# A hybrid attention block on one core: first token tile loaded first, products on a tile of zeros ahead of the first real ones, and an order planned anew

## The chip, the cores and the metric

One core of a Trainium2 chip runs the whole layer in one launch. The metric is device time in microseconds (us), the median of three runs. PE is TensorE, ACT ScalarE, DVE VectorE, POOL GpSimd, and SP the SyncE queue, from which all DMAs of this kernel are issued.

## The reference, cut to what matters

The input x has 1024 tokens of width 1024, in float32.

```python
h = rms_norm(x, norm_pre_g)
proj = h @ w_in            # sb_q, sb_k, sb_v, sb_gate, c_q, c_kv, k_rope, mla_gate
sb_o  = stick_breaking_attention(sb_q, sb_k, sb_v)        # 8 heads of 64, strictly causal
sb_y  = head_rms_norm(sb_o) * silu(sb_gate)
mla_o = latent_attention(...)                             # 8 heads, low rank q and kv, rotary part
mla_y = head_rms_norm(mla_o) * silu(mla_gate)
y = concat(sb_y, mla_y) @ w_out
x = x + rms_norm(y, norm_post_g)
x = x + rms_norm(p @ w_ple) * sigmoid(x @ w_ple_gate + b_ple_gate)
```

## The kernel before, in words

**Arithmetic.** Each float32 operand of a large product is split into a rounded high part and the rest, and a product is three PE passes: high by high, high by low, low by high. The products are mostly 128x512. The 1024 tokens are eight tiles of 128.

**The head.** `HEAD` (line 67) lists the first loads: `v0` to `v3` are four slabs of 512 KB of the value columns of `w_in` (`first`, line 936, then `load_split`, line 838, which also splits them), `x0` to `x2` are token tiles of 512 KB, and `g0` is the gain row `norm_pre_g` (4 KB). Lines 984 to 990 spread the gain row over 128 partitions by products with a tile of ones (`PE` into `ps_t`, `ACT.copy` into `gb["pre"]`) and do `x_norm(0)` and `x_tr(0)`. `x_norm` (line 859) is a square with a sum on ACT, a scale on DVE, a power on POOL, then the multiplication by the inverse root and the gain: on DVE alone for tiles below `EARLY` (line 866), on DVE and POOL from there on. `x_tr` (line 873) is eight PE transposes and the split of the result into `hh` and `hl`. `xv_gen` (line 947) then multiplies a token tile by the four slabs: 24 products into one PSUM bank of the three under the tag "a". The products for the queries and keys of the first head pair (`qk0_gen`, line 1027) follow.

**The middle.** `SEQ` (line 60) is the order in which head pairs are worked, `FILL0` (line 61) that of the projections woven between them, `RATES` (line 56) how many of those are spent for each stretch of attention. In `sb_rows` (line 1263) one row tile of the stick-breaking attention takes a product of every second element on POOL if its number `qi` is in `PAIRS` (lines 63 and 1283), otherwise on DVE.

**The tail.** `TAIL` (line 55) is the order of the last stage: `o` is an output projection with its norm, `w` loads and combines the gate weights, `x` and `a` load and transpose the new residual, `e` is the gated step for two token tiles, with seven products of half-size matrices in place of eight.

**How the order is made.** Nothing is issued when it is written down. The `Recorder` (line 333) notes every operation with the tiles that it reads and writes, a priority and a duration by formula (`cost`, line 461). The priority is the place in the recording, plus `SHIFT` of the piece that the operation belongs to (line 387; a piece begins at each `R.piece`), plus `LOW` (line 53) for background work, plus `R.bias` (`-URGENT` in the head, `-AHEAD` for attention scores). `schedule` (line 517) is a list planner: at each step it takes for an engine the ready operation of lowest priority, with `LAT` (line 510) added between a producer and a reader on another engine. It also holds durations doubled for PE until a stretch before was busy enough (lines 660 to 665). `FLIP` (line 224) names operations that are moved to another engine, and `SPLITS` (line 66, read by `choice`) says for groups of operations whether DVE or POOL does them. `issue` (line 698) then emits all operations in the planned order, and each engine works through its own list in that order, whatever the chip does.

The line of nearly all instructions in the profile is L730, in `issue`, so that rows are told apart by their tiles: `t` and `a` are PSUM banks, `u`, `f` and `h` SBUF tiles.

```python
prio=self.turn() + (LOW if self.low else 0) + self.bias
```

Of the kernel before, what the change touches and what calls it, by code (L numbers as in the profile page):

```python
# [15 lines left out]
BF16 = mybir.dt.bfloat16  # L16
# [31 lines left out]
def f(ap):  # L48
# [4 lines left out]
LOW = 336  # L53
TICK = 10240.0 / 3.0
TAIL = ("o4", "w1", "w2", "o5", "a4", "o6", "w3", "x1", "x0", "x2", "e4", "a0", "e0", "a6", "x3", "e6", "a2", "e2")
RATES = (4.934, 9.256, 4.735, 4.518, 3.1, 1.436, 0.789, 0.703, 2.078, 0.654, 0.413, 0.788, 0.259, 0.582, 0.786, 1.784)
URGENT = 56
EARLY = 4
LATER = 5
SEQ = ((0, 0), (1, 0), (6, 0), (4, 0), (7, 0), (2, 0), (0, 1), (3, 0), (3, 1), (2, 1), (5, 0), (7, 1), (5, 1), (4, 1), (1, 1), (6, 1))  # L60
FILL0 = ("x4", "x5", "l0", "x6", "x7", "q1", "c0", "b1", "r3", "t0", "lrv0", "g3", "rope0", "r0", "r1", "g4", "q2", "r2", "q3", "g6", "g0", "g1", "g2", "g7", "ple0", "g5")
N1 = 3
PAIRS = (0, 1, 2, 3)
ON_POOL = (0, 1, 2, 3)
LOWS = ("g", "q", "ple", "x", "b", "c", "t", "l")
SPLITS = (1, 0, 0, 1, 0, 1, 1, 1, 0, 1, 1, 1, 1, 1, 0, 1, 1, 0, 1, 0, 1, 1, 1, 0, 0, 1, 1, 1, 0, 0, 0, 1, 0, 0, 0, 1, 0, 0, 1, 0, 0, 1, 1)
HEAD = ("v0", "x1", "x0", "g0", "v3", "v1", "v2", "x2")
AHEAD = 52

SHIFT = {  # L70
# [662 lines left out]
def block_kernel(ctx, tc, x, p, positions, norm_pre_g, w_in, q_norm_g, w_uq, kv_norm_g, w_ukv,  # L733
# [3 lines left out]
    R = Recorder(nc)  # L737
# [52 lines left out]
    ones = const([1, 128], "ones")  # L790
    POOL.memset(ones, 1.0)
    nhalf = const([128, 8], "nhalf")
    POOL.memset(nhalf, -0.5)
    hpi = const([128, 1], "hpi")
    POOL.memset(hpi, HALF_PI)
    g_sb, g_mla = const([128, 4], "g_sb"), const([128, 4], "g_mla")
# [991 lines left out]
```

## Time and profile before

| what | value |
|---|---|
| median of 3 runs | 774.36 us (774.33 to 775.73) |
| the profiled execution | 774.4 us |
| its span, first to last instruction | 772.6 us |
| PE busy | 754.5 us, 98% of the span |
| DVE / ACT / POOL busy | 81% / 50% / 45% |

The profile is of one execution. Its busy times are unions of the instructions' spans, and matmul ends are modelled, so that a busy PE is not yet a PE at its full rate: the count of instructions in a stretch, or the time of a known number of them, tells the rate. The idle time of an engine is given with what ended it. The profiled execution differs from the median by 0.04 us, and 1.8 us of it lie outside the span.

### The profile page before, as it was taken

Reading aid. Unit: us, or ns where it says so; the run is one execution under the profiler, and the core shown is the slowest. Engines: PE = TensorE matmul, PEld = TensorE weight load, DVE = VectorE, ACT = ScalarE, POOL = GpSimd, SP = SyncE. Lnnn points to the kernel's source line nnn. Section 1 sums busy time; section 2 is a strip of 40 time slices with the busy share of each in tenths; the row PEclk is TensorE's granted clock in tenths of the full one; section 3 lists DMA queues with packets and bytes.
Section 4 is the critical chain, followed back from the end, with each engine's and each line's share of the span. In section 5 each row is a group of like instructions: output and inputs, shape, how many; then the busy total and the mean of one; then the engine's idle time right before and its main releaser. Section 6 shows DMA issues by size and latency. Waiting matters only on the chain.

```text
span 772.6 us, 11778 instructions
## 1 busy us (share of the span) xinstructions
PE 754.5 (98%) x3912; PEld 621.5 (80%) x3912; DVE 624.1 (81%) x1184; ACT 384.9 (50%) x898; POOL 346.6 (45%) x315
## 2 busy tenths in 40 slices
PE   6999999999999999999999899999999999999997
PEld 4887889878788878888788788888888888778886
DVE  5876334499867877788888899999899998888996
ACT  6315123333443586565646768776776642433211
POOL 4445111102312258878884712342275114468664
PEclk9999999999999999999999999999999999999999
DMA  9644460269995844566356588686734475172242
GB/s 329 201 171 139 145 213 5 77 218 354 330 341 190 275 155 143 167 206 189 110 184 225 187 290 260 216 302 223 240 116 154 166 254 178 60 268 87 94 150 82
DMA packets 101966, 148.69 MB, mean 192 GB/s; under 512 B 7441, under 2 KB 55057, under 8 KB 101906
## 3 DMA queue, kind: packets, MB, share of 16 engines
q1 hardware_dynamic: 101906, 147.95, 57.4%
q8 instruction: 31, 0.51, 0.3%
q14 instruction: 29, 0.24, 0.1%
HBM read 101.26 MB, written 46.66 MB: 191 GB/s over the span
## 4 chain that ended last, share of the span: by engine, by line
PE 84%; DVE 7%; DMA 4%; ACT 2%; issue 1%; POOL 1%; SPq 1%; POOLq 0%; ACTq 0%; DVEq 0%
PE a L730 58%; PE t L730 26%; DVE u L730 4%; DVE f L730 2%; ACT u L730 1%; DMA u<-k_d 1%; DMA u<-in_w_ple_gate_dram 1%; DMA u<-q_d 1%; DMA u<-in_x_dram 1%; DMA f<-in_positions_dram 1%; DMA q_d<-f 1%; SPq L730 1%; DVE nm L730 1%; ACT f L730 0%; POOL u L730 0%
## 5 line engine op out<-in xcount | busy, mean ns | idle before, releaser
L730 POOL TENSOR_TENSOR u<-u,u 128x512 f32<-128x512 f32 (+16 forms) x134 | 200.5, 1512 | 153.3 <-DVE u L730 64.0
L730 PE MATMUL a<-h,f 128*128 128x512 f32 x864 | 242.1, 405 | 0.0
L730 PEld LDWEIGHTS a<-h,f 128*128 128x128 f32 x864 | 155.2, 189 | 26.8 <-DVE f L730 0.6
L730 DVE TENSOR_TENSOR u<-t,u 128x512 fp32r<-128x512 f32 (+4 forms) x284 | 150.6, 556 | 13.7 <-ACT u L730 10.0
L730 PE MATMUL t<-u,u 128*128 128x512 f32 (+4 forms) x580 | 154.4, 370 | 1.9 <-DMA u<-q_d 0.5
L730 PE MATMUL a<-u,u 128*128 128x512 f32 (+2 forms) x524 | 136.7, 371 | 0.5 <-DVE u L730 0.5
L730 PE MATMUL t<-ident,u 128*128 128x128 f32 x792 | 125.8, 276 | 2.4 <-DVE u L730 2.4
L730 ACT ACTIVATE u<-t 128x512 f32<-128x512 f32 (+5 forms) x208 | 91.0, 509 | 67.7 <-PE t L730 57.8
L730 PEld LDWEIGHTS t<-u,u 128*128 128x128 f32 x580 | 103.4, 189 | 23.2 <-DVE u L730 4.3
L730 ACT CAST u<-t 128x512 fp32r<-128x512 f32 (+3 forms) x187 | 85.6, 495 | 71.0 <-PE t L730 35.3
L730 PE MATMUL a<-h,u 128*128 128x512 f32 (+1 forms) x492 | 118.3, 390 | 0.4 <-DVE u L730 0.4
L730 PEld LDWEIGHTS t<-ident,u 128*128 128x128 f32 x792 | 97.8, 142 | 24.9 <-DVE u L730 7.0
L730 PEld LDWEIGHTS a<-h,u 128*128 128x128 f32 x492 | 90.0, 188 | 21.3 <-issue 1.0
L730 PEld LDWEIGHTS a<-u,u 128*128 128x128 f32 x524 | 93.1, 188 | 17.2 <-DVE u L730 2.2
L730 ACT ACTIVATE u<-t,nms 128x384 f32<-128x384 f32 (+4 forms) x96 | 55.3, 581 | 42.3 <-DVE nms L730 35.3
L730 DVE TENSOR_TENSOR_SCAN u<-u 128x64 f32<-128x64 f32 (+6 forms) x64 | 59.1, 934 | 20.6 <-ACT u L730 20.4
L730 DVE TENSOR_TENSOR u<-u,u 128x512 f32<-128x512 f32 (+13 forms) x91 | 73.2, 820 | 2.0 <-ACT u L730 1.1
L730 DVE TENSOR_TENSOR u<-a,u 64x512 f32<-64x512 f32 (+4 forms) x75 | 47.8, 649 | 15.6 <-ACT u L730 9.7
L730 DVE TENSOR_REDUCE nm<-t 128x1 f32<-128x384 f32 (+4 forms) x96 | 51.6, 545 | 2.1 <-PE t L730 1.3
L730 POOL TENSOR_TENSOR rs<-ms,nhalf 128x8 f32<-128x8 f32 x16 | 27.7, 1731 | 57.0 <-DVE ms L730 37.5
L730 ACT ACTIVATE f<-a 128x512 bf16<-128x512 f32 (+3 forms) x64 | 34.3, 538 | 36.7 <-PE a L730 32.1
L730 PE MATMUL a<-u,h 128*128 128x512 f32 x192 | 49.8, 406 | 0.0
(110 smaller groups left out, 795.5 us busy)
## 6 DMA issues: line engine op xcount, KB each, us to landing
u<-q_d SPq DMA_DIRECT2D x64, 256.0 KB, 4.7
u<-k_d SPq DMA_DIRECT2D x16, 512.0 KB, 5.3
u<-v_d SPq DMA_DIRECT2D x16, 512.0 KB, 4.5
u<-in_w_ple_gate_dram SPq DMA_DIRECT2D x16, 512.0 KB, 5.4
f<-in_w_in_dram SPq DMA_DIRECT2D x14, 512.0 KB, 5.0
v_d<-u SPq DMA_DIRECT2D x12, 512.0 KB, 4.1
f<-in_x_dram SPq DMA_DIRECT2D x9, 512.0 KB, 4.6
k_d<-u SPq DMA_DIRECT2D x9, 512.0 KB, 3.9
```

The costliest lines, as they stand in the source:

```text
L730: x["fn"](*[place(a) for a in x["args"]], **{k: place(a) for k, a in x["kw"].items()})
```

## The change

The head list begins with `x0` and the gain row. A tile of zeros `still` (128x512, bf16) is set by DVE, and ahead of the head 20 products of it go into a PSUM bank that nothing reads; their priority number is raised by 150, so that the planner puts them where PE has nothing else that is ready. In the planner the delay from a landed DMA to its reader goes from 620 to 900 ns (650 to 950 for PE and POOL). With it all of the order's tables are other ones: `SHIFT` throughout, `FLIP` (225 entries before, 250 after), `TAIL`, `SEQ` (one swap), `FILL0`, `RATES`, `LOW`, `URGENT`, `EARLY`, `AHEAD`, `PAIRS` and `SPLITS` (entries 9, 13, 19 and 22; 13 is not read by any line). The arithmetic of the result is the same.

```diff
-LOW = 336
+LOW = 377
-TAIL = ("o4", "w1", "w2", "o5", "a4", "o6", "w3", "x1", "x0", "x2", "e4", "a0", "e0", "a6", "x3", "e6", "a2", "e2")
-RATES = (4.934, 9.256, 4.735, 4.518, 3.1, 1.436, 0.789, 0.703, 2.078, 0.654, 0.413, 0.788, 0.259, 0.582, 0.786, 1.784)
-URGENT = 56
-EARLY = 4
+TAIL = ("w1", "w2", "w3", "o4", "o5", "x0", "x2", "a4", "o6", "e4", "x1", "a0", "e0", "x3", "a6", "e6", "a2", "e2")
+RATES = (4.934, 9.256, 4.735, 4.518, 3.1, 1.642, 0.698, 0.666, 2.078, 0.654, 0.413, 0.788, 0.304, 0.522, 0.229, 3.217)
+URGENT = 83
+EARLY = 3
-SEQ = (... (5, 0), (7, 1), (5, 1), (4, 1), (1, 1), (6, 1))
-FILL0 = ("x4", "x5", "l0", "x6", "x7", "q1", "c0", "b1", "r3", "t0", "lrv0", "g3", "rope0", "r0", "r1", "g4", ...)
+SEQ = (... (5, 0), (5, 1), (7, 1), (4, 1), (1, 1), (6, 1))
+FILL0 = ("l0", "x4", "x5", "x6", "x7", "q1", "c0", "r3", "b1", "t0", "lrv0", "g3", "g4", "r0", "rope0", "r1", ...)
-PAIRS = (0, 1, 2, 3)
+PAIRS = (0, 1, 3)
-HEAD = ("v0", "x1", "x0", "g0", "v3", "v1", "v2", "x2")
-AHEAD = 52
+HEAD = ("x0", "g0", "v0", "x2", "x1", "v1", "v3", "v2")
+WARM = (20, 150)
+AHEAD = -3
...
-           ("POOL", "DVE"): 65.0, ("POOL", "POOL"): 102.0, ("POOL", "SP"): 55.0, ("SP", "PE"): 650.0,
-           ("SP", "ACT"): 620.0, ("SP", "DVE"): 620.0, ("SP", "POOL"): 650.0, ("SP", "SP"): 620.0}
+           ("POOL", "DVE"): 65.0, ("POOL", "POOL"): 102.0, ("POOL", "SP"): 55.0, ("SP", "PE"): 950.0,
+           ("SP", "ACT"): 900.0, ("SP", "DVE"): 900.0, ("SP", "POOL"): 950.0, ("SP", "SP"): 900.0}
...
+    still = const([128, 512], "still", BF16)
+    DVE.memset(still, 0.0)
...
+    R.piece("warm")
+    R.bias = WARM[1]
+    idle = ps_a()
+    for _ in range(WARM[0]):
+        mm(idle, still[:, 0:128], still, start=True, stop=True)
+    R.bias = 0
     for item in HEAD:
         R.piece(item)
         first(item)
```

## Rows read from the trace of the kernel before

**Rows 1.** The page's first part: busy time, share of the span and instructions of each engine.

```profile
span 772.6 us, 11778 instructions
PE 754.5 (98%) x3912; PEld 621.5 (80%) x3912; DVE 624.1 (81%) x1184; ACT 384.9 (50%) x898; POOL 346.6 (45%) x315
```

**Rows 2.** Busy time by stage: stretch in us, its length, then busy us (instructions) of PE, PEld, DVE, ACT and POOL, the granted clock of PE, the DMA engines' share, GB/s.

```profile
0.00:6.00 6.00, 0.01 (x1) 0.04 (x1) 0.43 (x1) 2.11 (x2) 1.36 (x11) 1.00 0.68 217
6.00:10.50 4.50, 3.74 (x4) 1.12 (x4) 1.71 (x5) 3.57 (x7) 3.89 (x3) 1.00 1.04 407
10.50:15.80 5.30, 5.29 (x20) 4.66 (x21) 5.30 (x8) 3.51 (x6) 0.42 (x1) 1.00 1.02 394
15.80:40.00 24.20, 24.20 (x118) 19.93 (x117) 20.86 (x36) 11.03 (x19) 12.04 (x10) 1.00 0.68 212
40.00:280.00 240.00, 237.64 (x1200) 197.34 (x1199) 160.13 (x374) 91.42 (x242) 61.43 (x72) 1.00 0.60 203
280.00:360.00 80.00, 80.00 (x450) 65.50 (x449) 65.17 (x94) 54.42 (x126) 67.43 (x63) 1.00 0.55 169
360.00:400.00 40.00, 39.25 (x209) 31.62 (x208) 32.96 (x45) 20.00 (x42) 33.80 (x20) 1.00 0.51 166
400.00:440.00 40.00, 38.37 (x211) 31.42 (x210) 35.77 (x61) 26.43 (x65) 24.86 (x23) 1.00 0.58 195
764.75:772.60 7.85, 2.69 (x23) 2.49 (x22) 4.61 (x9) 1.36 (x3) 2.13 (x2) 0.84 0.27 100
```

**Rows 3.** What PE waited for in the whole span (waits of over 0.15 us): us in total, times, longest.

```profile
PE t L730 <- DMA u<-in_norm_pre_g_dram: 6.0, 1, 6.0
PE t L730 <- DVE u L730: 2.8, 5, 1.2
PE a L730 <- DVE u L730: 0.9, 2, 0.5
PE a L730 <- DVE f L730: 0.6, 1, 0.6
PE t L730 <- DVE f L730: 0.6, 2, 0.3
PE t L730 <- DMA u<-q_d: 0.5, 1, 0.5
PE t L730 <- ACT u L730: 0.3, 1, 0.3
PE a L730 <- ACT f L730: 0.3, 1, 0.3
PE t L730 <- DMA u<-k_d: 0.3, 1, 0.3
```

**Rows 4.** Instructions in order of time, 0 to 14 us: start, length, engine, operation, tiles, form, count, and the idle time before with what ended it.

```profile
0.73 0.20 POOL masks.py:197 MEMSET ident<- 128x128 f32 x1 [0.29 <-POOLq L1769]
0.74 0.44 SPq L730 DMA_DIRECT2D u<-in_w_in_dram  x1
1.24 0.46 SPq L730 DMA_DIRECT2D u<-in_x_dram  x1
1.45 0.43 DVE L730 CAST eye<-ident 128x128 bf16<-128x128 f32 x1 [1.45 <-POOL ident masks.py:199]
1.74 0.33 SPq L730 DMA_DIRECT2D u<-in_norm_pre_g_dram  x1
2.12 0.35 SPq L730 DMA_DIRECT2D u<-in_x_dram  x1
5.17 1.04 ACT L730 CAST u<-u 128x1024 fp32r<-128x1024 f32 x1 [3.16 <-DMA u<-in_w_in_dram]
6.44 1.06 ACT L730 ACTIVATE u<-u 128x1024 bf16<-128x1024 f32 x1 [0.22 <-DMA u<-in_x_dram]
7.76 1.06 ACT L730 ACTIVATE u<-u 128x1024 bf16<-128x1024 f32 x1 [0.17 <-DMA u<-in_x_dram]
8.81 0.56 ACT L730 COPY u<-t 128x512 f32<-128x512 f32 x1
9.71 2.63 DVE L730 SCALAR_TENSOR_TENSOR u<-u,sr,u 128x512 f32<-128x512 f32 x3
```

**Rows 5.** The same view for PE alone, 0 to 32 us.

```profile
5.99 3.75 PE L730 MATMUL t<-u,ones 1*128 1x512 f32 x4 [5.99 <-DMA u<-in_norm_pre_g_dram]
10.51 1.97 PE L730 MATMUL t<-ident,u 128*128 128x128 f32 x8 [0.77 <-DVE u L730]
24.05 3.04 PE L730 MATMUL a<-u,h 128*128 128x512 f32 x12
```

**Rows 6.** Busy time of the instructions on the tile `ident` alone (the transposes), in four stretches that each hold eight of them; the columns are PE, PEld, DVE, POOL, granted clock, DMA share, GB/s.

```profile
13.31:15.02 1.71, 1.71 (x8) 1.50 (x7) 0.00 (x0) 0.00 (x0) 1.00 1.05 396
23.27:24.05 0.78, 0.78 (x8) 0.78 (x7) 0.00 (x0) 0.00 (x0) 1.00 0.00 0
```

**Rows 7.** Groups of PE instructions by form from 10.5 to 15.5 us: busy us, mean ns, idle before.

```profile
L730 PE MATMUL a<-u,h 128*128 128x512 f32 x4 | 2.3, 686 | 0.0
```

**Rows 8.** Groups by form over the whole span, POOL and DVE: busy us, mean ns of one, idle before and what ended it.

```profile
L730 POOL TENSOR_TENSOR u<-u,u 128x448 f32<-128x448 f32 x7 | 13.3, 1900 | 2.2 <-ACT u L730 2.2
L730 POOL TENSOR_TENSOR u<-u,u 128x192 f32<-128x192 f32 x4 | 3.0, 748 | 3.2 <-ACT u L730 3.2
L730 DVE TENSOR_TENSOR u<-u,u 128x448 f32<-128x448 f32 x1 | 0.6, 600 | 0.0
L730 DVE TENSOR_TENSOR u<-u,u 128x192 f32<-128x192 f32 x1 | 0.4, 359 | 0.4 <-ACT u L730 0.4
L730 POOL TENSOR_TENSOR u<-u,u 128x1024 f32<-128x1024 f32 x2 | 5.3, 2632 | 2.1 <-DVE u L730 2.1
L730 DVE TENSOR_TENSOR u<-u,u 128x512 f32<-128x512 f32 x35 | 28.9, 842 | 0.6 <-ACT u L730 0.3
L730 DVE TENSOR_TENSOR u<-a,u 128x512 f32<-128x512 f32 x31 | 20.7, 684 | 5.5 <-PE a L730 4.0 <-ACT h L730 1.1 <-ACT u L730 0.2
```

More of the change, by code (lines that the diff above doesn't have):

```diff
@@ L52 @@
 NU, NF = 28, 10
-LOW = 336
+LOW = 377
 TICK = 10240.0 / 3.0
-TAIL = ("o4", "w1", "w2", "o5", "a4", "o6", "w3", "x1", "x0", "x2", "e4", "a0", "e0", "a6", "x3", "e6", "a2", "e2")
-RATES = (4.934, 9.256, 4.735, 4.518, 3.1, 1.436, 0.789, 0.703, 2.078, 0.654, 0.413, 0.788, 0.259, 0.582, 0.786, 1.784)
-URGENT = 56
-EARLY = 4
+TAIL = ("w1", "w2", "w3", "o4", "o5", "x0", "x2", "a4", "o6", "e4", "x1", "a0", "e0", "x3", "a6", "e6", "a2", "e2")
+RATES = (4.934, 9.256, 4.735, 4.518, 3.1, 1.642, 0.698, 0.666, 2.078, 0.654, 0.413, 0.788, 0.304, 0.522, 0.229, 3.217)
+URGENT = 83
+EARLY = 3
 LATER = 5
-SEQ = ((0, 0), (1, 0), (6, 0), (4, 0), (7, 0), (2, 0), (0, 1), (3, 0), (3, 1), (2, 1), (5, 0), (7, 1), (5, 1), (4, 1), (1, 1), (6, 1))
-FILL0 = ("x4", "x5", "l0", "x6", "x7", "q1", "c0", "b1", "r3", "t0", "lrv0", "g3", "rope0", "r0", "r1", "g4", "q2", "r2", "q3", "g6", "g0", "g1", "g2", "g7", "ple0", "g5")
+SEQ = ((0, 0), (1, 0), (6, 0), (4, 0), (7, 0), (2, 0), (0, 1), (3, 0), (3, 1), (2, 1), (5, 0), (5, 1), (7, 1), (4, 1), (1, 1), (6, 1))
+FILL0 = ("l0", "x4", "x5", "x6", "x7", "q1", "c0", "r3", "b1", "t0", "lrv0", "g3", "g4", "r0", "rope0", "r1", "q2", "r2", "q3", "g6", "g0", "g1", "g2", "g7", "ple0", "g5")
 N1 = 3
-PAIRS = (0, 1, 2, 3)
+PAIRS = (0, 1, 3)
 ON_POOL = (0, 1, 2, 3)
 LOWS = ("g", "q", "ple", "x", "b", "c", "t", "l")
-SPLITS = (1, 0, 0, 1, 0, 1, 1, 1, 0, 1, 1, 1, 1, 1, 0, 1, 1, 0, 1, 0, 1, 1, 1, 0, 0, 1, 1, 1, 0, 0, 0, 1, 0, 0, 0, 1, 0, 0, 1, 0, 0, 1, 1)
-HEAD = ("v0", "x1", "x0", "g0", "v3", "v1", "v2", "x2")
-AHEAD = 52
+SPLITS = (1, 0, 0, 1, 0, 1, 1, 1, 0, 0, 1, 1, 1, 0, 0, 1, 1, 0, 1, 1, 1, 1, 0, 0, 0, 1, 1, 1, 0, 0, 0, 1, 0, 0, 0, 1, 0, 0, 1, 0, 0, 1, 1)
+HEAD = ("x0", "g0", "v0", "x2", "x1", "v1", "v3", "v2")
+WARM = (20, 150)
+AHEAD = -3
 SHIFT = {
[151 rows of a table removed]
[159 rows of a table added]
 }
 FLIP = (
[12 rows of a table removed]
[13 rows of a table added]
 )
```

335 rows, old and new, of tables (FLIP, SHIFT) are left out of this document.

## The prediction, made before the changed kernel was run

> **What bounds the kernel now.** I read the engines' totals first: PE is busy 754.5 of 772.6 us, and no other engine over 81% [rows 1]. So there are 18 us at most to take out, plus time in which a busy PE runs below its rate. The stages say where they lie [rows 2]: 6.7 us ahead of 10.5 us, 5.2 us after 764.75 (the last sums and stores, which follow PE's last product), and some 6 us in all between; from 15.8 to 40 us and from 280 to 360 us PE is never idle. The list of PE's waits agrees: 6.0 us for the gain row's DMA at the start, then many short ones, most ended by DVE [rows 3].
>
> The head in order of time [rows 4, 5]: SP issues a weight slab at 0.74, `x1` at 1.24, the gain row at 1.74, `x0` at 2.12. The three loads of 512 KB free their first readers on ACT at 5.17, 6.44 and 7.76: one every 1.3 us, while the DMA engines are full [rows 2]. `x0`, which starts the chain (square, scale, power, multiplication, transposes), is the third of them. Its first transpose runs at 10.51, 2.75 us after its square began.
>
> That PE is busy from 10.5 to 15.8 us hides a second loss. The granted-clock column reads 1.00 there, but eight transposes take 1.71 us at 13.31 and 0.78 us at 23.27 [rows 6], and four 128x512 products 2.3 us against 12 in 3.04 us later [rows 5, 7]. I go by the durations: until about 15.8 us PE works at 1.2 GHz, after that at 2.4. Before the rise it had worked without a break since 10.51; the four products of the gain row (5.99 to 9.74) and the gap of 0.77 us behind them had not brought it.
>
> **The change part by part.**
>
> *Half-rate work made full-rate.* 16 transposes take 1.97 + 1.71 us with waits; I count 2 x (1.71 - 0.78) = 1.9 us [rows 6]. The four products: 2.3 - 4 x 0.25 = 1.3 us, of which about 0.5 is the first ones' wait for operands, so 0.8. If PE is at full rate when it reaches them: **-2.7 us** (bounds 0 and -3.2).
>
> *`x0` first.* It would land where the first load did, 5.17 in place of 7.76, and the same 2.75 us of chain would give a first transpose at 7.9. But the multiplication also needs the gain row's products: their row is there by 5.99, the first half takes two products (1.9 us at half rate, 0.95 at full) and an ACT copy of 0.56, then about 0.75 of DVE [rows 4, 5]: 8.3 to 9.2. So by the data, a gain of 1.3 to 2.2 us.
>
> *The 20 products of zeros.* They wait for a memset on DVE, which can run from 0.73, as the other engines do, so I let them start at 1.2. No row has a 128x512 bf16 product. Bounds for one: 0.25 us (float32r, full rate) and 0.94 (the one-row float32 products) [rows 5]; nearest is the first, doubled while at half rate. As before the rise came after 5.3 us of unbroken work, I put it at 6.5: about 11 products at 0.5 by then, 9 at 0.25, then the gain row's four at 0.47: they would end at 10.7. The Trainium skill (TensorE: Matmul & The Clock Gate, Part 1) gives 0.427 and 0.216 us for a product of this size at the two rates; by these figures the end would be 9.9, an estimate, and no row here shows such a product. PE takes its list in order, so whichever zeros stand ahead of the transposes hold them. Between 8.3 (data) and 10.7 (queue) I take 9.7, nearer to the queue, since nothing else is ready for PE by then and the planner will have put nearly all 20 there: **-0.8 us** (bounds -2.2 and +0.3).
>
> *`x1` later.* It goes from the second 512 KB to about the fifth, so to a landing near 10.3 and transposes near 13. Between 9.7 and there PE has 0.8 us of transposes and some 1.5 us of products with the first slab, and those for `x2`, which lands earlier. I charge **+0.3 us** (bounds 0 and 1.3). Later loads stay in the saturated DMA stream and are not late: PE is the last to finish with them up to 40 us [rows 2].
>
> *Longer DMA delay in the planner.* It moves transfers ahead of their use. The waits it aims at are those for `q_d` and `k_d`, 0.8 us [rows 3]: I take **-0.4 us** (bounds -0.8 and, if it spreads uses apart, +1).
>
> *`PAIRS`.* Products with `qi` 2 go from POOL to DVE: 7 x 1.90 + 4 x 0.75 = 16.3 us less on POOL, 7 x 0.60 + 4 x 0.36 = 5.6 us more on DVE [rows 8]. Most lie between 280 and 440 us, where POOL is up to 84% busy and DVE 81 to 89% [rows 2]. I cost them at nothing: DVE has 26 us free there. If that cover goes they cost up to 5.6 us. The Trainium skill (SBUF — State Buffer, Who interferes with whom) says that a DVE operation with two SBUF inputs and a GpSimd one that reads SBUF hold one port in turn; by that 16.3 us of holding go and 5.6 come, and the edit would be a gain, at most the 2.4 us that PE idles there. The trace leans that way: 0.84 us for two SBUF inputs, 0.68 with one in PSUM [rows 8].
>
> *The rest together, nothing.* `EARLY` puts 2.6 us of POOL behind `x3`, needed only by the fourth token tile; four low parts of gate weights go from DVE to POOL; two splits of small weights change engine: PE waits 1.5 us on such tiles in the whole span [rows 3]. The tail's last three steps are the same, so the 7.85 us after 764.75 stay [rows 2]. `SHIFT`, `FLIP`, `SEQ`, `RATES`: PE's work is the same, and nothing in the trace tells which short wait goes or comes; I take 0, with 4 us to either side.
>
> Sum: -2.7 - 0.8 + 0.3 - 0.4 = -3.6 us on the profiled execution's 774.4, whose difference to the median (774.36) is nothing: **770.8 us**.
>
> **The rivals.**
>
> *A, the new order also closes waits in the middle.* PE waits listed behind the head come to 5.5 us (12.3 less 6.0 and 0.77) [rows 3]. Closing 4 of them beyond the above gives 766.8. For: most are single waits for DVE of under 1.2 us, which another order can remove. Against: nothing in the diff names one.
>
> *B, the zeros stand in the way.* If the clock rises only as the last of them ends (1.2 + 20 x 0.5 = 11.2, then 1.9 us for the gain row), the transposes start at 13.1: 2.6 us later, which returns the 2.7 us: 774.3, the same. Zeros that leave the clock as it is come out near this or, with the transposes at half rate too, some 4 us above it. For: PE's list is in order, and before the clock came late. The Trainium skill (TensorE: Matmul & The Clock Gate, Part 2, step 1) says that only weight loads are pulled ahead, matmuls stay in program order; no row of before has ready work behind waiting products, so none tests it.
>
> *C, slower: DVE becomes the bound between 280 and 440 us.* The 5.6 us moved onto it come out ahead of PE there: 770.8 + 5.6 = 776.4. It decides once PE's waits for DVE in this stretch exceed some 6 us; they are about 2.4 us of idle PE now, all after 360 us. For: DVE ends most of PE's waits. Against: 26 us of free DVE time, and POOL's relief.
>
> **How the numbers follow.** Forecast 0.52 (its own range 768.5 to 772.5, from the head's bounds), A 0.18, B 0.15, C 0.13, and 0.02 for a larger gain than A. A measurement of this kernel can tell about 0.2%, 1.5 us, from no change. Faster: the forecast, A and the rest, 0.72; same: B, 0.15; slower: C, 0.13. The range goes from 766.2, just past A, to 775.6, past B; it leaves out C and a larger gain.
>
> **What would show it.** Right: the first loads' reader on ACT is a square, at about 5.2; products of zeros fill PE from about 1.2; transposes start between 8.3 and 10.7 and eight take 0.8 us from the first; PE has no gap over 0.5 us until 40 us; from there the same products run some 3.5 us earlier. The forecast is wrong if the first eight transposes take 1.7 us, or start after 11 (B), if PE's idle time between 280 and 440 us is over 6 us (C), or if the idle time between 40 and 660 us moves by more than 2 us (A, or an order that fits the chip worse).

## The result, and the profile after

The changed kernel takes **777.76 us** (median of 6 runs, 776.45 to 779.32) against 774.56 (6 runs, 774.02 to 775.73) of the kernel before on the same chip: a ratio of 1.0042, 95% interval 1.0027 to 1.0056. That is 3.2 us slower, where 3.6 us faster was forecast, and outside the range. The profiled execution took 777.18 us, 0.6 less than the median, 775.4 of them in the span. One execution of one experiment below (`a_f0`, 1059 us where its others lie between 776.7 and 780.9) was far slower than the rest and is left out of its ratio.

The totals of after, the lines that answer to [rows 1]:

```profile
span 775.4 us, 11804 instructions
PE 760.4 (98%) x3932; PEld 622.3 (80%) x3932; DVE 636.5 (82%) x1206; ACT 388.9 (50%) x898; POOL 315.6 (41%) x297
```

PE is busy 5.9 us longer. The 20 products of zeros take 7.3 us of it, so the real products take 1.4 us less. DVE has 12.4 us more, POOL 31.0 less.

Stages of after, to set beside [rows 2] (columns as there):

```profile
0.00:6.00 6.00, 4.81 (x12) 1.75 (x13) 0.27 (x1) 2.50 (x3) 1.31 (x11) 1.00 0.67 205
6.00:10.50 4.50, 4.41 (x14) 1.45 (x12) 2.31 (x4) 1.92 (x5) 0.97 (x1) 1.00 1.04 416
10.50:15.80 5.30, 4.41 (x19) 3.02 (x20) 4.90 (x8) 5.30 (x10) 1.07 (x2) 1.00 1.07 359
15.80:40.00 24.20, 23.60 (x117) 18.77 (x116) 23.17 (x36) 12.57 (x24) 16.98 (x10) 1.00 0.70 238
280.00:360.00 80.00, 79.66 (x449) 65.11 (x449) 71.27 (x105) 54.59 (x129) 58.95 (x56) 1.00 0.59 185
400.00:440.00 40.00, 38.39 (x205) 30.68 (x204) 36.10 (x59) 23.67 (x55) 22.88 (x20) 1.00 0.62 199
```

The head is filled (4.81 and 4.41 us busy, where [rows 2] has 0.01 and 3.74), but 1.5 us of idle PE have come between 10.5 and 40 us, where before had none; between 280 and 360 us, the place of rival C, 0.34 us of PE is idle with DVE 89% busy. From 400 to 440 us PE is as busy as before (38.39 and 38.37 us), yet has 205 products to show for it where before has 211 (of mixed sizes): busy time alone does not tell its progress.

Chosen lines of the head of after in order of time (start, length, engine, operation, tiles, form, count, idle time before and what ended it), to set beside [rows 4, 5]:

```profile
0.74 0.44 SPq L740 DMA_DIRECT2D u<-in_w_in_dram  x1
1.19 7.31 PE L740 MATMUL a<-still 128*128 128x512 bf16 x20 [1.19 <-DVE still L740]
1.24 0.45 SPq L740 DMA_DIRECT2D u<-in_x_dram  x1
1.74 0.33 SPq L740 DMA_DIRECT2D u<-in_norm_pre_g_dram  x1
5.08 1.04 ACT L740 CAST u<-u 128x1024 fp32r<-128x1024 f32 x1 [2.76 <-DMA u<-in_w_in_dram]
6.35 1.06 ACT L740 ACTIVATE u<-u 128x1024 bf16<-128x1024 f32 x1 [0.22 <-DMA u<-in_x_dram]
8.43 1.98 PE L740 MATMUL t<-u,ones 1*128 1x512 f32 x4
9.59 0.59 ACT L740 COPY u<-t 128x512 f32<-128x512 f32 x1 [2.08 <-PE t L740]
11.07 1.45 PE L740 MATMUL t<-ident,u 128*128 128x128 f32 x8 [0.66 <-DVE u L740]
12.61 3.60 PE L740 MATMUL a<-u,h 128*128 128x512 f32 x12
13.35 0.43 SPq L740 DMA_DIRECT2D u<-in_w_in_dram  x1
16.14 1.09 PE L740 MATMUL t<-ident,u 128*128 128x128 f32 x8
```

A weight slab is still the first transfer and `x0` the second; `x0`'s square starts at 6.35, and before had one at 6.44. The zeros hold the gain row's products until 8.43 (5.99 in [rows 5]); behind them ACT waits 2.08 us for its copy. The first transpose runs at 11.07, later than the 10.51 of before. The clock is up: eight transposes take 1.45 us with a wait inside, then 1.09, where [rows 5, 6] have 1.97 and 1.71.

PE's waits of after, to set beside [rows 3] (us in total, times, longest):

```profile
PE t L740 <- ACT u L740: 2.0, 5, 0.8
PE a L740 <- DVE still L740: 1.2, 1, 1.2
PE a L740 <- ACT f L740: 1.1, 3, 0.7
PE t L740 <- DMA u<-q_d: 1.0, 1, 1.0
PE t L740 <- DVE u L740: 0.8, 2, 0.7
PE t L740 <- DVE f L740: 0.8, 2, 0.4
PE a L740 <- DVE f L740: 0.7, 2, 0.4
PE a L740 <- ACT u L740: 0.5, 2, 0.3
```

The 6.0 us for the gain row and most of the 2.8 us for DVE `u` are gone. Besides the 1.2 us at the start, until the tile of zeros is set, many short waits stand in their place: 3.6 us of the 6.9 shown are ended by ACT, for which PE had waited 0.6 us in all.

Waits alone don't place the loss, so I also count PE's progress: each real product counts with the median step of its form in before, from its start to the next one's (a 128x512 one 0.233 us; zeros count nothing), summed up to a moment. The lead is that sum minus the sum of before at the same moment, in us; the total of both kernels is some 736. A row is good to some 0.3 us, since whole products are counted, and it is from one profiled execution. Some of these are extremes of their kernel: `a_f0` and `a_f12` were profiled 2.8 and 2.6 us above their medians, `a_q`, `b_f20` and `b_x0b` 1.3 to 1.7 below, which shows in the right-hand columns. Names without a meaning yet are those of the experiments below.

```
                               at 40   200   230   380   480   720   760 us
after                           -0.5   1.1   0.4   1.6  -0.6  -3.1  -3.0
order of after,  a_f0            0.2   2.2  -1.1   0.2  -2.8  -6.2  -6.7
                 a_f12           0.6   2.7  -0.7   0.5  -2.4  -4.9  -5.3
                 a_q             0.9   2.1   2.7   3.8   0.5  -1.7  -1.6
                 a_pairs        -0.2   1.1   0.7   1.5  -1.8  -5.3  -5.7
                 a_ple          -0.2   1.7   0.3   1.5  -1.6  -4.4  -4.3
                 a_norm          0.4   2.1   1.6   2.6   2.5  -0.8  -0.7
order of before, b_f20           1.7   2.9   3.1   2.3   3.0   2.3   2.3
                 b_x0b           1.8   2.4   2.9   3.0   3.7   2.8   2.7
                 b_ple           0.9   0.2   0.7   0.4   1.2   0.5   0.5
                 b_norm          0.9   0.7   0.0   0.0   2.0   2.3   2.3
```

After is behind at 40 us, ahead by 1.6 at 380, and loses 2.2 us up to 480 and 2.5 more up to 720. Runs of one kernel scatter by 0.7 to 8 us, so that a difference of rows is trusted here only where all rows of an order show it. From 380 to 720 us the lead falls by 3.4 to 6.8 in all seven rows of after's order. In those of before's order, with the four profiles that are not in the table (`b_f11`, `b_split`, `b_pairs`, `b_x0`), it moves by no more than some 1.2 either way, and by 2.3 upward in `b_norm`, which does less work. At 40 us, on the other hand, a difference under 1 us means little: `b_ple` and `b_norm` have the head of before unchanged and are 0.9 ahead there, with 24 products between 10.5 and 15.8 us where before had 20.

### The profile page after: what moved, and what is told of

Read it like the earlier page. It is cut to its first block, busy times and chain, and to the rows that moved or that the text cites. A ratio compares the mean times of both kernels' runs of the same rounds, so it can differ in the third digit from the quotient of the medians.

```text
span 775.4 us, 11804 instructions
## 1 busy us (share of the span) xinstructions
PE 760.4 (98%) x3932; PEld 622.3 (80%) x3932; DVE 636.5 (82%) x1206; ACT 388.9 (50%) x898; POOL 315.6 (41%) x297
## 4 chain that ended last, share of the span: by engine, by line
PE 75%; DVE 12%; DMA 4%; issue 4%; ACT 3%; POOL 1%; SPq 1%; POOLq 0%; ACTq 0%; DVEq 0%
PE a L740 54%; PE t L740 21%; DVE u L740 8%; DVE f L740 2%; ACT u L740 2%; DMA u<-in_w_ple_gate_dram 2%; DMA u<-q_d 1%; ACT f L740 1%; DVE h L740 1%; POOL u L740 1%; DMA v_d<-u 1%; DVE nm L740 1%; DMA u<-k_d 1%; SPq L740 1%; DMA q_d<-f 0%
## 5 line engine op out<-in xcount | busy, mean ns | idle before, releaser
L740 POOL TENSOR_TENSOR u<-u,u 128x512 f32<-128x512 f32 (+14 forms) x133 | 188.5, 1431 | 154.6 <-ACT u L740 68.0
L740 DVE TENSOR_TENSOR u<-t,u 128x512 fp32r<-128x512 f32 (+4 forms) x284 | 151.2, 554 | 13.6 <-ACT u L740 11.3
L740 PE MATMUL t<-u,u 128*128 128x512 f32 (+4 forms) x576 | 156.3, 371 | 1.9 <-DMA u<-q_d 1.0
L740 PE MATMUL a<-u,u 128*128 128x512 f32 (+2 forms) x525 | 130.9, 369 | 2.1 <-ACT f L740 0.9
L740 ACT CAST u<-t 128x512 fp32r<-128x512 f32 (+3 forms) x176 | 81.8, 496 | 75.3 <-PE t L740 47.5
L740 PEld LDWEIGHTS t<-ident,u 128*128 128x128 f32 x792 | 95.8, 140 | 26.1 <-ACT u L740 5.6
L740 DVE TENSOR_TENSOR u<-u,u 128x512 f32<-128x512 f32 (+17 forms) x100 | 83.2, 846 | 9.3 <-ACT u L740 7.4
L740 ACT ACTIVATE u<-t,nms 128x384 f32<-128x384 f32 (+5 forms) x96 | 55.3, 581 | 38.3 <-DVE nms L740 32.1
L740 ACT ACTIVATE f<-a 128x512 bf16<-128x512 f32 (+2 forms) x64 | 34.1, 534 | 73.6 <-PE a L740 71.2
L740 DVE TENSOR_REDUCE nm<-t 128x1 f32<-128x384 f32 (+5 forms) x96 | 51.7, 544 | 1.2 <-ACT u L740 0.3
L740 DVE TENSOR_TENSOR f<-a,f 128x512 f32<-128x512 f32 (+2 forms) x54 | 34.3, 643 | 20.9 <-ACT f L740 18.0
```

The lines of the kernel that those rows point to most:

```text
L740: x["fn"](*[place(a) for a in x["args"]], **{k: place(a) for k, a in x["kw"].items()})
```

## The experiments

Times are medians, and a ratio is taken against runs of the kernel before on the same chip on the same occasion (its medians lie between 774.32 and 775.31 us). In the short diffs, `order` is the list that `issue` walks; "frozen" means that nothing is planned anew.

### What the zeros are worth in the order of before

`b_f20` and `b_f11` put 20 and 11 zeros ahead of the frozen order of before; `b_split` puts 11 ahead of and 9 behind the gain row's products.

```diff
+            zeros(20)        # b_f20; 11 in b_f11 and b_split
 ...
+                if i == 24:  # b_split only
+                    zeros(9)
```

Expected of `b_f20`:

> The kernel before in its own order, with the memset and 20 products of zeros put at the very front of PE's list and nothing else changed. Theory 1 (the clock is worth its 2.7 us where PE is the bound, and the zeros cost what they hold back): the gain row's products wait until 8.4, transposes start near 11.1 in place of 10.5, at full rate: -2.7 + 0.6, about 772.4 us. Theory 2 (the head is bound by the arrival of loads and their splits, so a faster PE waits): 774.5, as before.

Measured: 773.81 us, ratio 0.9987 (0.9973 to 1.0001). Its PE:

```profile
1.19 7.04 PE L707 MATMUL a<-still 128*128 128x512 bf16 x20 [1.19 <-DVE still L705]
8.16 1.98 PE L737 MATMUL t<-u,ones 1*128 1x512 f32 x4
10.81 1.45 PE L737 MATMUL t<-ident,u 128*128 128x128 f32 x8 [0.67 <-DVE u L737]
12.80 1.09 PE L737 MATMUL t<-ident,u 128*128 128x128 f32 x8
```

The transposes come nearly as late as in after (10.81 and 11.07 us), at full rate, and PE is 1.7 us ahead at 40 us, which stays to the end of this profile. By the times, the zeros are worth about 1 us, at the edge of what can be told.

Expected of `b_f11`:

> As the run with 20, but 11 products of zeros, which end at about 5.9, when the gain row is there. Theory 1: transposes at 10.5 as before, and full rate from there if the gain row's products keep the clock up: 771.9 us. Theory 2: 774.5. If the clock does not rise by 10.5 with 11: 774.5 too, and the transposes take 1.7 us for eight.

Measured: 774.59 us, 0.9994 (0.9977 to 1.0011). The gain row's products are on time, but the clock falls again: it is granted at 0.50 from 10.3 to 13.5 us, and the first eight transposes take 1.97 us. Expected of `b_split`:

> The kernel before in its own order, with 11 products of zeros ahead of the gain row's products and 9 behind them, in the hole of about 2 us ahead of the transposes. Theory 1 (zeros pay where they keep the clock up and hold nothing): transposes at 10.5 as before, at full rate, PE's progress at 40 us ahead of before by 2 to 2.5 us: 772.2 us. If the head's gain is given back in the middle of this order: 774.4.

Measured: 773.67 us, 0.9991 (0.9974 to 1.0007). The gain row's products, and a stage behind them (columns as in [rows 2]):

```profile
5.90 1.95 PE L739 MATMUL t<-u,ones 1*128 1x512 f32 x4 [0.42 <-DMA u<-in_norm_pre_g_dram]
8.20:11.50 3.30, 3.30 (x10) 1.38 (x9) 2.66 (x5) 1.57 (x4) 1.87 (x3) 0.50 1.05 411
```

The clock is at half (1.2 GHz) from 8.2 to 11.5 us, although PE is busy all of that time; before it, PE had waited 0.42 us and done the gain row's one-row products. So PE being busy did not keep the clock up here, and filling around the gain row did no better than 20 zeros in front.

### What the order costs without the zeros

`a_f0` and `a_f12` keep the frozen order of after, with none or 12 of its zeros.

```diff
+        warm = [i for i in order if self.threads[self.ins[i]["chunk"]] == "warm"]
+        order = [i for i in order if i not in warm[0:]]    # a_f12: warm[12:]
```

> The changed kernel in its own order, with the 20 products of zeros left out. Theory 1: the gain row's products run from 6.0, transposes some 0.8 us earlier, but at half rate to about 15.5: 777.8 + 1.5 to 2, near 779.5 us. Theory 2: the head is bound by loads and splits: 777.3 to 778.3, no difference.

> The changed kernel in its own order, with 12 of the 20 products of zeros. Theory 1: they end at 6.3, the gain row's products follow at once, transposes 1 to 1.5 us earlier than 11.07 and at full rate: 776.5 us. Theory 2: splits and loads come as before, so PE waits later instead: 777.8.

Measured: `a_f0` 778.06 us, 1.0047 (1.0034 to 1.0061); `a_f12` 776.88, 1.0025 (1.0014 to 1.0037). So all of the change but the zeros, the order for short, costs 3.7 us; its 20 zeros give back next to nothing, and 12 of them 1 to 2 us, with intervals that touch. Both profiles show one thing more, a wait that grows when PE comes early. `a_f12` around it:

```profile
212.00:216.00 4.00, 2.28 (x11) 1.57 (x9) 2.27 (x5) 1.90 (x3) 0.00 (x0) 1.00 0.96 328
216.00:220.00 4.00, 3.35 (x11) 2.91 (x12) 0.98 (x5) 0.40 (x2) 0.00 (x0) 0.57 1.08 375
```

PE waits 2.36 us for `q_d`, whose row comes at 216.65, as in after (216.93, 0.96 us of wait); the DMA engines are full. Then the clock is granted at 0.57 on average, that is at half for most of the stretch. The lead of 2.7 us at 200 is gone at 230.

`a_q` moves the two transfers that stand ahead of that `q_d` load behind it, with 12 zeros:

```diff
+        for i in (1818, 1339):
+            order.remove(i)
+            order.insert(order.index(1755) + 1, i)
```

> The run with 12 of the 20 zeros, with two transfers of 256 KB (an attention value load that is first read some 40 us later, and the store of a gate) moved in SP's order behind the query loads that PE waits for near 216 us. Theory Q (a full DMA stream in which those queries stand too late sets the time of this stretch and takes the head's gain): PE's wait for q_d there falls from 2.4 to about 1.1 us, the clock stays up, total 1.3 to 3 us less than the 776.9 of that run: 774.5 us. Rival (what is won there is lost again at 400 to 480 us): 776.9.

Measured: 777.05 us, 1.0028 (1.0016 to 1.0040). In its profile the wait is gone and PE never idle from 212 to 220 us, but by the median nothing was gained over `a_f12`. Its lead falls by 3.3 us between 380 and 480 and 2.2 more up to 720, much as in the other rows of this order that have the norm.

### The pair products

`a_pairs` moves the 13 products of every second element that after has on DVE for `qi` 2 to POOL, where before had 11 of them; `b_pairs` moves 11 of them from POOL to DVE in the order of before (its expectation says ten).

```diff
+        for x in self.ins:    # a_pairs; b_pairs: POOL to DVE
+            if x["op"] == "tensor_tensor" and x["eng"] == "DVE" and x["args"][0].shape[-1] in (192, 448) ...:
+                x.update(eng="POOL", fn=self.POOL.eng.tensor_tensor)
```

> The changed kernel in its own order, with the products of qi 2 that now run on DVE (8 of 448 and 5 of 192 elements, some 6.9 us of DVE) given back to POOL. Theory C (DVE's load bounds PE between 280 and 480 us): the waits there fall and the time by 1.5 to 3 us, 775.5. Rival (the moved products are covered): 777.8, or slower where the POOL form is late for the next step.

> The order of before with one edit of the change alone: ten products of every second element in the row tiles with qi = 2 go from POOL to DVE, at their old place in the order. Theory (the edit is a gain in itself, because a DVE operation is held up while POOL works on SBUF, as undoing it in the order of after cost 2 to 3 us): PE's waits for DVE and ACT between 280 and 440 us get shorter, and the time is 772.5 to 773.5. Rival C of the prediction in its own place (DVE is the bound there): DVE gets 4 to 5 us more work between 280 and 440 us, and the time is 776 or more. A third (neither, PE has enough cover): 774.5.

Measured: `a_pairs` 779.93 us, 1.0066 (1.0053 to 1.0079); `b_pairs` 775.09, 0.9998 (0.9984 to 1.0012). In before's order the edit is worth nothing, as the prediction had it. In after's order, undoing it costs some 2 us (the intervals of `a_pairs` and after touch). Either way DVE's extra work did not cost the time: rival C falls. Whether POOL holds DVE up is not settled. The scans of 128x448, first in after, then in `a_pairs`:

```profile
L740 DVE TENSOR_TENSOR_SCAN u<-u 128x448 f32<-128x448 f32 x8 | 10.2, 1274 | 0.3 <-ACT u L740 0.3
```

```profile
L744 DVE TENSOR_TENSOR_SCAN u<-u 128x448 f32<-128x448 f32 x8 | 12.7, 1592 | 0.3 <-ACT u L744 0.3
```

They slow by 0.32 us each when the products go to POOL. But in `b_pairs`, where 11 leave POOL, they take 1.216 us, in before 1.141: the other direction.

### Old tables, the new planner's delays

`b_lat900` gives the planner of before the DMA delays of after and leaves all its tables.

```diff
-           ... ("SP", "PE"): 650.0, ("SP", "ACT"): 620.0, ...
+           ... ("SP", "PE"): 950.0, ("SP", "ACT"): 900.0, ...
```

> The kernel before with the planner's delay behind a DMA at 900 in place of 620 ns, and its own tables. Theory F (the tables of order shifts fit only the planner that they were made with): the order falls apart, 10 to 30 us slower, above 785 us. Theory P (the longer delay is itself better or worse on the chip, the tables carry over): within 3 us of 774.5.

Measured: one run, 793.09 us. An order planned anew from tables that were not chosen for it cost 18 us in this run, far beyond the scatter of before's runs; its lead, counted as above, is 0.2 us at 280, -4.2 at 380 and -13.5 at 720, so that the loss is spread over the middle. What a table entry is worth hangs on the planner it was set with, so that this run puts no price on "the longer delay" by itself.

### x0 really first

`b_x0` issues `x0` and the gain row ahead of the first slab, and moves parts of its chain ahead, in before's order with 14 zeros.

```diff
+        ahead([10, 11], 6)         # x0, gain row ahead of the slab
+        ahead([26, 27, 28], 7)     # square, scale, power of x0 ahead of the slab's split
+        ahead([23], 43)            # a copy of the gain ahead of x1's square
```

> The order of before with eleven zeros ahead of the gain row's products and three behind the first two of them, and with x0 really the first transfer: x0 and the gain row are issued ahead of the first weight slab, x0's square, scale and power ahead of that slab's split, the gain's first copy ahead of x1's square. Theory (the head was worth what was forecast, and the change's order did not carry it out): x0's square starts at about 5.1 us instead of 6.4, the first transposes at 9.0 to 9.6 instead of 10.5 and at full rate, PE is 2 to 2.5 us ahead of before at 40 us, and the time is 772.5, about 1 us below the kernel with the zeros in two groups in before's own order (773.7). Rival (after x0 the slabs set the pace): the first slab lands at 7.7 instead of 5.1, the products wait for it, PE is at most 1.3 us ahead at 40 us, and the time is 773.7 or more.

Measured: 775.9 us, 1.0013 (1.0000 to 1.0026). The edit did not move the whole chain: `x0`'s square starts at 4.24, but I had left the gain's copies on ACT behind the slab's split (8.83), and `x0`'s multiplication on DVE behind a slab and `x1` (11.81). The first transpose runs at 12.61, and PE is 2.4 us behind before at 40 us.

`b_x0b` moves the whole chain:

```diff
+        first = [10, 11, 6, 9, 15, 26, 27, 28, 22, 23, 24, 25, 29, 30, 7, 8, 31, 32, 33, 34, 37, 38, 39, 40,
+                 35, 36, 43, 16, 44, 45, 41, 42, 64, 65, 66, 67, 68, 69, 46]
+        order = setup + first + [i for i in order if i not in setup + first]
 ...
+                zeros({24: 3, 40: 3, 64: 7}.get(i, 0))
```

> The order of before with x0 really first and its whole chain moved with it: x0 and the gain row ahead of the first slab on SP; square, both copies of the gain and the first split of the transposes ahead of x1's square on ACT; x0's multiplication ahead of everything on DVE; the six products with the first slab ahead of x1's transposes on PE; 11, 3, 3 and 7 zeros in the gaps. Theory (x0's place in the stream is worth what was forecast, 0.8 us, and full rate on top): first transpose at 8.0 to 8.5 us, PE 2.3 to 3 us ahead of before at 40 us, 772 us. Rival (the slabs that come 1.3 us later and the splits on DVE and ACT give the start back): first transpose just as early, but PE waits between 9 and 15 us, is 1 to 1.8 us ahead at 40 us, no more than with the zeros alone in before's own order (1.65), and the time is 773.5 or more.

Measured: 773.27 us, 0.9986 (0.9972 to 1.0000). Its head in order of time:

```profile
0.74 0.39 SPq L743 DMA_DIRECT2D u<-in_x_dram  x1
3.97 1.06 ACT L743 ACTIVATE u<-u 128x1024 bf16<-128x1024 f32 x1 [1.95 <-DMA u<-in_x_dram]
7.47 1.05 ACT L743 CAST u<-u 128x1024 fp32r<-128x1024 f32 x1
7.62 1.45 PE L743 MATMUL t<-ident,u 128*128 128x128 f32 x8
9.37 0.58 PE L743 MATMUL a<-u,h 128*128 128x512 f32 x1
9.79 1.69 PE L712 MATMUL a<-still 128*128 128x512 bf16 x7
11.12 1.51 PE L743 MATMUL a<-u,h 128*128 128x512 f32 x5
13.59 0.66 PE L743 MATMUL t<-ident,u 128*128 128x128 f32 x4 [0.96 <-DVE u L743]
```

The rival holds, with the time 0.2 us under its bound. The transposes start at 7.62, 2.9 us earlier than before and at full rate, but between 9 and 13.6 us PE has six real products, and its lead at 40 us is 1.8 us, as with zeros alone (1.7). `b_x0b` and `b_f20` have the lowest ratios of kernels that do all the work; neither is told from 1 with certainty.

### What the middle waits for

`a_ple` and `b_ple` leave out the eight scalings of 128x1024 in the branch of `p`, 5.9 us of DVE; `a_norm` and `b_norm` leave out that branch's whole norm (squares on ACT, powers, scalings).

```diff
+        cut = [i for i in order if self.ins[i]["op"] == "tensor_scalar" and self.ins[i]["eng"] == "DVE"
+               and self.ins[i]["args"][0].shape[-1] == 1024 and "ple" in self.threads[self.ins[i]["chunk"]]]
+        order = [i for i in order if i not in cut]    # a_norm, b_norm: all that use hss, hsm or hsr there
```

> The order of after without the eight scalings of 128x1024 in the branch of p, 5.9 us of DVE work between 400 and 520 us; rms_norm(p @ w_ple) lacks its scale and the rest is computed as before. Theory D (in the order of after DVE's load sets PE's waits between 400 and 520 us): PE's waits there for DVE f, DVE u and, through DVE, for ACT u and ACT f fall by over half, the lead over before at 480 us rises from -0.6 to about +1.5, and the time is 774.5 to 775.5 where after has 777.8. Theory E (single chains in a frozen order set them, and DVE has slack between): the waits stay within 0.5 us, and the time is 777 or more.

> The order of before without the same eight scalings; rms_norm(p @ w_ple) lacks its scale and the rest is computed as before. It shows what the same relief is worth in the order of before. Theory D: DVE is as full there, but the order covers it better: 773 to 774, less than half of what after gets back. Theory E: 774.5, no change. If both kernels fall by the same, DVE's load costs both alike and doesn't explain the difference.

> The order of after without the norm in the branch of p: its 16 squares of 128x512 on ACT with their sums (about 0.8 us each, 12.6 us of ACT), its scale and eps (some 16 small DVE operations), eight powers on POOL and the eight scalings on DVE are left out; p @ w_ple is stored with its gain alone. All this lies between 400 and 500 us. Theory ACT (load on ACT in this stretch makes the waits that the order of after has and before has not): PE's waits for ACT there go, and the time falls by 2 us or more, to 775.8 or less. Theory E (single short chains in the frozen order, which have no norm in them): the waits for attention's transposes stay, and the time falls by under 1 us, to 777 or more.

> The order of before without the same norm. Theory ACT: before has its waits covered, so it falls by less than 1 us, 773.5 to 774.5. Theory E: it falls by as much as after does. If both fall by 2 us or more, the load of this stretch costs both orders alike and does not explain the difference.

Measured: `a_ple` 778.08 us, 1.0041 (1.0028 to 1.0054), what after has; `b_ple` 773.95, 0.9987 (0.9976 to 0.9999). DVE's busy time falls by only 4.0 and 1.6 us in these two profiles, but after's time does not fall at all, so that this load is not what after loses by: theory D falls. `a_norm` 775.01, 0.9997 (0.9986 to 1.0009), and `b_norm` 772.24, 0.9967 (0.9956 to 0.9979): 3.5 and 2.6 us less than their kernels. The load of this branch costs both orders, and between the two versions without it there are still 0.30%. In the leads, the loss of `a_norm` between 380 and 480 us is 0.1 instead of 2.2 to 3.3, but `b_norm` gains 2.0 there too. From 480 to 720 us `a_norm` loses 3.3, no less than after (2.5). PE's waits there, of after and of `a_norm`:

```profile
PE t L740 <- ACT u L740: 0.5, 2, 0.3
PE a L740 <- ACT u L740: 0.5, 2, 0.3
PE a L740 <- DVE u L740: 0.3, 1, 0.3
PE a L740 <- ACT f L740: 0.2, 1, 0.2
PE t L740 <- DVE t L740: 0.2, 1, 0.2
```

```profile
PE t L742 <- ACT u L742: 1.0, 2, 0.8
PE a L742 <- ACT u L742: 0.5, 2, 0.3
PE a L742 <- DVE u L742: 0.3, 1, 0.3
PE a L742 <- ACT f L742: 0.2, 1, 0.2
PE t L742 <- DVE t L742: 0.2, 1, 0.2
```

The same waits, on the same tiles, one of them longer. They go with the order, not with the load that was removed.

The listed time is less than a wait costs. A 128x512 product lasts some 0.39 us in the trace, but the next one starts 0.233 us after it, so that PE loses some 0.16 us more at each wait than its idle time, and a shorter wait does not show as idle at all. After's seven waits of 1.7 us cost some 2.8 us by this estimate and the two of before there (0.6 us) some 0.9; that is 1.9 of the 2.5 us of lead. The idle time by itself would mislead, as `b_f20` has as much of it and more products done:

```profile
480.00:720.00 240.00, 238.31 (x1253) 197.26 (x1252) 216.13 (x408) 132.09 (x289) 93.41 (x78) 1.00 0.59 195
480.00:720.00 240.00, 238.37 (x1260) 197.95 (x1259) 219.47 (x392) 130.83 (x289) 104.07 (x82) 1.00 0.56 187
```

The first line is after, the second `b_f20` (columns as in [rows 2]).

## Why the prediction was wrong, point by point

**`x0` first: the first step that failed.** The prediction took the first place in `HEAD` for the first place in SP's queue, and the load at 2.12 us for `x0`. `HEAD` only sets the order of recording; the priorities, with `SHIFT`, set that of issue. In before `x0` is the load at 1.24, its square the one at 6.44: its multiplication starts at 9.71 [rows 4], before the second of the two powers on POOL is done (both run from 8.61 to 10.20), so that it can't belong to the later square. In after it is again the second load, with its square at 6.35. So the step "5.17 in place of 7.76" did not take place. `b_x0b` makes it in before's order: the transposes start 2.9 us earlier, but the lead at 40 us (1.8) is no more than with zeros alone (1.7), and the ratios are the same (0.9986 and 0.9987). There it was worth nothing that can be told.

**The zeros.** The first transpose was put at 9.7 with bounds 8.3 and 10.7; it came at 11.07, 0.6 later than before, so the term was +0.6 instead of -0.8. The mechanism was the one named, the queue: the zeros ended at 8.43, and the gain row's four products took 1.98 us. The estimate with the Trainium skill's figures (TensorE: Matmul & The Clock Gate, Part 1) was 9.9 for the end of the gain row's products; the trace has 10.41. The Trainium skill's 0.427 us for a product at half rate agrees with the trace: 12 zeros start in the first 4.81 us, so that a step is 0.40 to 0.44. The Trainium skill's rule on order (the same page, Part 2, step 1) agrees with the trace too: the gain row's products, ready at about 6, did not pass the zeros.

**Half-rate work made full-rate.** The mechanism held in this execution: 1.45 and 1.09 us for the transposes. It does not hold in each one: in `a_norm`, with the same head, the clock was granted at 0.50 from 11.7 to 14.9 us. The forecast of 2.7 us is in before's order a lead of 1.7 and about 1 us of time (`b_f20`). In after's order it was spent on the next point.

**"Later loads are not late."** The last slab is issued at 13.35 where SP had issued it at 6.44, because SP, behind an issue at 7.79, waited 4.0 us for DVE to be done with a slab whose buffer the next token tile takes (next issue 12.98). That split stands on DVE behind `x0`'s multiplication, which waits for the gain's copy, so that the zeros delay it too: without them (`a_f0`) the last slab is issued at 12.30, and the rest is the order's. PE is idle 1.5 us between 10.5 and 40 us. "3.5 us earlier from there" was 0.5 us later. That includes `x1`, for which 0.3 us were charged.

**The longer DMA delay, -0.4.** Wrong sign in the profile: the wait for `q_d` went from 0.5 to 1.0 us, and to 2.1 and 2.4 in `a_f0` and `a_f12`. It came with the whole new order, so that the delay's own share is not shown.

**`PAIRS`, nothing.** Right in the order of before (`b_pairs`). Rival C had the right sign and a time only 1.4 us off (776.4), but its cause is refuted, so that this was luck. Rival B's condition did not hold either: the clock was up before the zeros ended, or the gain row's products would not have taken 1.98 us where before had 3.75.

**"`SHIFT`, `FLIP`, `SEQ`, `RATES`: I take 0, with 4 us to either side."** The step that decided. The order alone costs 3.7 us (`a_f0`); after's lead falls by 4.7 us between 380 and 720. The prediction wrote down 4 us to either side, but gave only the gain a rival (A), and cut the range at 775.6 where this bound, on the forecast, reached 774.8, and on B 778.3. Shown: the loss is in every profile of this order and in none of before's; it is not the zeros, not the pair products, not the 5.9 us of scalings on DVE, and behind 480 us, by one profile, not the norm's load either. Open: which of the tables made it, or whether the planner's delay did. Each wait is a different short chain (ACT `u`, ACT `f`, DVE `f`), and I only argue that it is single instructions in the wrong place in ACT's and DVE's queues; no run moved them.

## What to carry to other kernels

Take the order of transfers from the queue's rows, and tell equal transfers apart by their readers; a list in the source is not the order of issue. An order planned anew is an edit with a price of its own, of either sign: give it a rival on each side, as large as the bound you write down. And an earlier start counts only if the second and third operands come earlier too: price a head by what PE has done at its end, not by its first product.

## What the hardware showed that was not expected

- **The clock rises at different times after the same start.** Zeros always begin at 1.19 us, yet 11 of them took 4.87 us in `b_f11` and 3.86 in `b_x0b`, where the clock came up among them. Part of the scatter between runs may come from it; no run tells.
- **One-row products and the clock.** In `b_split` it was at half from 8.2 to 11.5 us with PE 100% busy, after a wait of 0.42 us and 1.95 us of the gain row's products. In `b_f20` and `b_x0b` the same four products, 1.98 us at full rate, did not bring it down, so that they alone don't explain it.
- **The same transfers in another order moved less.** With a slab first, 4 to 8 us move 410 GB/s; with `x0`, then the gain row, then the slab the rate is 310 (`b_x0b`) and 313 (`b_x0`), and in `b_x0` the slab's split waits for its DMA until 7.88. First before, then `b_x0b`:

```profile
4.00:8.00 4.00, 2.01 (x3) 1.00 (x4) 0.15 (x1) 2.43 (x4) 1.70 (x1) 1.00 1.03 410
```

```profile
4.00:8.00 4.00, 4.00 (x15) 1.55 (x14) 1.30 (x3) 2.71 (x5) 0.56 (x1) 1.00 0.94 310
```

No run tells whether the gain row's small transfer or something else makes the difference.
